# SBUF pools in another order, three small tiles filled up: where the matmul operands begin

## Chip, core and metric

The kernel runs on one core of one Trainium2 chip. Its time is the device time of one execution in microseconds (us), and a profiled execution gives a trace of the same program. TensorE is called PE here, and PEld is its loading of the stationary operand; VectorE is DVE, ScalarE is ACT, GpSimd is POOL, SyncE is SP.

## What is computed

One layer of a hybrid encoder trunk, for 1024 positions and a width of 1024, in float32:

```python
h = rms_norm(x, pre_norm_gain)
q, k, v, z_a, b_gate, c_gate, u, z_c = split(h @ w_in, 8)        # 8 x 512 columns
weights = softmax(q1 k1 + bias) - lam * softmax(q2 k2 + bias)    # 4 heads, block-causal, ALiBi
attn = rms_norm(weights @ v, subln_gain) * 0.2 * ... * silu(z_a)
conv_out = b_gate * conv3(c_gate * u) * silu(z_c)
mixed = concat(attn, conv_out) @ w_out
x = x + rms_norm(mixed, post_norm_gain)
e = rms_norm(p @ w_ple_proj, ple_norm_gain)
out = x + sigmoid(x @ w_ple_gate) * e
```

## The kernel before

Everything is held transposed: features lie on the 128 partitions and positions along the free dimension, in two halves of 512. A float32 product is made from three matmuls of type float32r: each operand is split into a high part (a rounded copy) and a low part (what the copy lost), and `mm3` (lines 93 to 96) adds high x high, high x low and low x high in one PSUM bank. `product` (line 123) runs it over the eight tiles of the contraction, 24 matmuls of 512 columns into one bank. In these the weights `w` are the stationary operand and the activations move: `hT` (the normalised input) in the input projection, whose banks are named `pj`; `mT` (the mixed groups) and `x1` (the residual stream) in the output projection and the gate, whose banks are named `o`. In the v projection it is the other way round: a slice of `hT` is stationary and the weights `wv` move, into `v`. Scores (`s`) have `qs` stationary and `ks` moving, in 256, 384 or 512 columns; `values` transposes the softmax weights on PE (`tpw`) and multiplies them as the moving `wt` with the stationary `vs` into `av`. `ple` is the projection of the per-layer embedding at the start.

The program has four parts in time. First x, p and the embedding weights are loaded and split and `ple` is made. Then come the first head's q and k and the v projection, whose results go through DRAM. Then, by the table `PLAN` and head by head, softmax on DVE and ACT alternates with further input projections on PE (gates and short convolutions). Last, `out_half` makes the output projection, `post_stat` and `post` the norm and the residual `x1`, half by half, and `gate_half` the gate and the output; the last `gate_half` goes in two pieces of 256 columns. DMAs are issued from SP; POOL makes the low parts of the weights (line 84). A scheduler orders the instructions of each engine from the order in which the code is written.

SBUF is given out by pools. A pool takes its place when it is opened, behind the pools that are open, and each tile takes its bytes per partition rounded up to a multiple of 32. So the start of a tile hangs on the sizes of all that lie before it. The pools, in the order of lines 49 to 55: `const` (identity, small constants, two rows `R` of scales), `hp` (16 buffers for hT, then mT, then x1), `mixp`, `tiny`, `rawp` (weights as loaded) and `wp` (weights split). Behind them the stages open and close their own: `qk` (qs, ks), `rowp`, `sp` and `s2` (wph, wpo, zero, pth, pto), `vp` (wv), `ap`, `a2` and `a3` (softmax weights, vs, wt), and in the last part `cp`, `c2`, `c4` and `wp2`. In `const`, before `hp`, lie tiles of 16, 64, 148, 4 and 128 bytes, which take 32, 64, 160, 32 and 128. In `mixp` the tile `gt` has 514 columns, 2056 bytes, and takes 2080; `lam_e` in `qk` has 8 bytes and takes 32.

Of the kernel before, what the change touches and what calls it, by code (L numbers as in the profile page):

```python
# [12 lines left out]
F32 = mybir.dt.float32  # L13
# [7 lines left out]
P = 128  # L21
# [4 lines left out]
HALF = 512  # L26
# [17 lines left out]
def hybrid_layer(ctx, tc, xT, pT, w_in, small, lams, w_out, w_ple, w_gate, outT):  # L44
    nc = tc.nc
    V, A, T, G = nc.vector, nc.scalar, nc.tensor, nc.gpsimd
    mult, add, sub = ALU.mult, ALU.add, ALU.subtract

    const = ctx.enter_context(tc.tile_pool(name="const", bufs=1))
    dram = ctx.enter_context(tc.tile_pool(name="dram", bufs=1, space=DRAM))  # L50
    hp = ctx.enter_context(tc.tile_pool(name="hp", bufs=16))
    mixp = ctx.enter_context(tc.tile_pool(name="mixp", bufs=1))
    tiny = ctx.enter_context(tc.tile_pool(name="tiny", bufs=3))
    rawp = ctx.enter_context(tc.tile_pool(name="rawp", bufs=3))
    wp = ctx.enter_context(tc.tile_pool(name="wp", bufs=3))
    ps_s = ctx.enter_context(tc.tile_pool(name="ps_s", bufs=3, space=PSUM))
    ps_a = ctx.enter_context(tc.tile_pool(name="ps_a", bufs=1, space=PSUM))

# [9 lines left out]
    ident = const.tile([P, P], F32, name="ident")  # L68
    make_identity(nc, ident)
    fold = const.tile([P, P], F32, name="fold")  # L70
    own = const.tile([P, 4], F32, name="own")
    nhalf = const.tile([P, 16], F32, name="nhalf")
    G.memset(nhalf, -0.5)
    sm = const.tile([P, 37], F32, name="sm")
# [67 lines left out]

    hT = operand("hT")
    mix = [[mixp.tile([P, HALF], F32, tag="mix", bufs=16, name=f"mix{k}_{n}") for n in range(2)] for k in range(KT)]
    gt = mixp.tile([P, HALF + 2], F32, name="gt")
    R = [const.tile([P, HALF], F32, name=f"R{n}") for n in range(2)]

    with ExitStack() as st:
        qk = st.enter_context(tc.tile_pool(name="qk", bufs=1))
        rowp = st.enter_context(tc.tile_pool(name="rowp", bufs=3))  # L150

        lam_in = mix[5][1][:, 0:256].rearrange("p (a b) -> p a b", a=4)
        lam_e = qk.tile([P, 2], F32, name="lam_e")
        nlam = qk.tile([P, 1], F32, name="nlam")

        def mixing_weight():
# [458 lines left out]
```

## Time and profile before

| | |
|---|---|
| median of three executions | 669.23 us (667.34 to 671.49) |
| the profiled execution | 670.35 us |
| its span, first to last instruction | 668.5 us |
| mean granted clock of TensorE in it | 0.992 of 2.4 GHz |

The span is what the trace shows; the profiled execution's own time is 1.85 us above it. Busy times are sums over the span for each engine. A matmul's end in the trace is modelled, and consecutive matmuls overlap there, so starts are to be read, not durations. The granted clock is 1.00 at 2.4 GHz and 0.50 at 1.2 GHz.

### The profile page before, as it was taken

What the parts mean: (1) busy time and instruction counts of PE and PEld (TensorE: products, weight loads), DVE (VectorE), ACT (ScalarE), POOL (GpSimd) and SP (SyncE); (2) the same over time, 40 slices, a digit from 0 to 9 for tenths busy, and PEclk for the clock granted to TensorE, in tenths of its full rate; (3) what the DMA queues carried; (4) which work ended last, traced back from release to release, by engine and by line L of the source; (5) the groups of instructions that cost most, each with busy time, mean ns of one, the idle gap of its engine ahead of it and who ended that gap; (6) DMA issues with size and microseconds to landing.
All of it is one profiled execution on the core that took longest, in us unless ns stands there. A gap on an engine that the chain in (4) does not pass through costs nothing.

```text
span 668.5 us, 8063 instructions
## 1 busy us (share of the span) xinstructions
PE 651.3 (97%) x2941; PEld 526.7 (79%) x2941; DVE 454.6 (68%) x828; ACT 241.7 (36%) x434; POOL 228.3 (34%) x115
## 2 busy tenths in 40 slices
PE   8999699999999999999999999999999999999996
PEld 5787478888888888888888888888888888877885
DVE  6959661479778786598834989618792189796333
ACT  6934441243443332344323334312541227231111
POOL 2046340032622354152351312425370187560000
PEclk9999899999999999999999999999999999999998
DMA  8966562300135001250012610113141024142222
GB/s 289 403 223 188 183 202 94 127 32 32 48 85 152 32 31 49 54 151 33 33 63 51 169 33 32 50 32 108 63 158 32 1 94 163 57 132 91 96 94 94
DMA packets 35654, 67.77 MB, mean 101 GB/s; under 512 B 3744, under 2 KB 12448, under 8 KB 35616
## 3 DMA queue, kind: packets, MB, share of 16 engines
q1 hardware_dynamic: 35616, 67.27, 30.7%
q8 instruction: 23, 0.38, 0.2%
q14 instruction: 15, 0.12, 0.1%
HBM read 48.38 MB, written 12.58 MB: 91 GB/s over the span
## 4 chain that ended last, share of the span: by engine, by line
PE 67%; DMA 11%; DVE 10%; issue 6%; POOL 5%; ACT 1%; SPq 0%; DVEq 0%; POOLq 0%
PE pj L94 12%; PE pj L96 12%; PE pj L95 12%; PE o L94 5%; PE o L96 5%; PE o L95 5%; PE s L232 5%; DMA e<-e_dram 4%; DMA out_dram<-e 3%; PE tpw L259 2%; POOL w L84 2%; PE v L94 2%; PE v L95 2%; PE v L96 2%; DMA mix<-in_xT 2%
## 5 line engine op out<-in xcount | busy, mean ns | idle before, releaser
L94 PE MATMUL pj<-hT,w 128*128 128x512 f32 x448 | 179.1, 400 | 0.6 <-ACT w L83 0.4
L96 PE MATMUL pj<-hT,w 128*128 128x512 f32 x448 | 178.1, 398 | 0.0
L95 PE MATMUL pj<-hT,w 128*128 128x512 f32 x448 | 177.9, 397 | 0.0
L84 POOL TENSOR_TENSOR w<-raw,w 128x1024 fp32r<-128x1024 f32 x42 | 106.8, 2549 | 202.3 <-ACT w L83 190.4
L94 PEld LDWEIGHTS pj<-hT,w 128*128 128x128 f32 x448 | 84.3, 188 | 19.3 <-ACT w L83 0.8
L96 PEld LDWEIGHTS pj<-hT,w 128*128 128x128 f32 x448 | 84.2, 188 | 18.6
L95 PEld LDWEIGHTS pj<-hT,w 128*128 128x128 f32 x448 | 84.2, 188 | 18.0
L240 ACT ACTIVATE p<-p,nm 128x128 f32<-128x128 f32 (+7 forms) x64 | 49.4, 772 | 73.9 <-DVE nm L236 63.3
L83 ACT CAST w<-raw 128x1024 fp32r<-128x1024 f32 x44 | 45.8, 1047 | 51.3 <-issue 35.2
L95 PE MATMUL o<-x,w 128*128 128x512 f32 (+1 forms) x136 | 52.1, 383 | 1.5 <-DVE x L84 1.5
L94 PE MATMUL o<-x,w 128*128 128x512 f32 (+1 forms) x136 | 52.2, 385 | 0.0
L96 PE MATMUL o<-x,w 128*128 128x512 f32 (+1 forms) x136 | 51.9, 381 | 0.0
L94 PE MATMUL o<-mT,w 128*128 128x512 f32 x128 | 51.1, 399 | 0.0
L96 PE MATMUL o<-mT,w 128*128 128x512 f32 x128 | 50.4, 395 | 0.0
L95 PE MATMUL o<-mT,w 128*128 128x512 f32 x128 | 50.2, 392 | 0.0
L232 PE MATMUL s<-ks,qs 128*128 128x512 f32 (+2 forms) x192 | 46.6, 347 | 0.5 <-issue 0.5
L236 DVE CUSTOM_DVE_ANT_0 p<-s,bias 128x512 f32<-128x512 f32 (+3 forms) x64 | 34.7, 565 | 9.6 <-PE s L232 5.6
L546 DVE SCALAR_TENSOR_TENSOR e<-e,sm,re 128x512 f32<-128x512 f32 x16 | 16.2, 1015 | 35.9 <-DMA e<-e_dram 35.9
L232 PEld LDWEIGHTS s<-ks,qs 128*128 128x128 f32 x192 | 33.3, 188 | 6.2 <-issue 0.9
L83 ACT CAST wt<-tpw 128x512 fp32r<-128x512 f32 (+3 forms) x48 | 20.7, 478 | 45.1 <-PE tpw L259 44.9
L84 DVE TENSOR_TENSOR wt<-tpw,wt 128x512 fp32r<-128x512 f32 (+3 forms) x48 | 25.2, 551 | 16.4 <-ACT wt L83 16.1
L555 ACT ACTIVATE tg<-o 128x512 f32<-128x512 f32 (+1 forms) x17 | 9.7, 572 | 65.6 <-PE o L96 63.0
(139 smaller groups left out, 1134.0 us busy)
## 6 DMA issues: line engine op xcount, KB each, us to landing
raw<-in_w_in SPq DMA_DIRECT2D x32, 512.0 KB, 3.9
mix<-in_xT SPq DMA_DIRECT2D x16, 256.0 KB, 5.9
e_dram<-e SPq DMA_DIRECT2D x16, 256.0 KB, 5.2
mix<-e_dram SPq DMA_DIRECT2D x16, 256.0 KB, 3.5
ks<-ks SPq DMA_DIRECT2D x16, 256.0 KB, 3.6
v_dram<-v SPq DMA_DIRECT2D x8, 512.0 KB, 3.1
vs<-v_dram SPq DMA_DIRECT2D x32, 128.0 KB, 2.8
raw<-in_w_out SPq DMA_DIRECT2D x8, 512.0 KB, 3.3
```

Of the source, the lines that this page charges most:

```text
L83: A.copy(out=hi, in_=src)
L84: (lo_eng or V).tensor_tensor(out=lo, in0=src, in1=hi.bitcast(F32), op=sub)
L94: T.matmul(out=ps, lhsT=ah, rhs=bh, start=first, stop=False)
L95: T.matmul(out=ps, lhsT=ah, rhs=bl, start=False, stop=False)
L96: T.matmul(out=ps, lhsT=al, rhs=bh, start=False, stop=last)
L232: T.matmul(out=banks[m][:, :nn], lhsT=s.qs[:, m, qi], rhs=s.ks[:, m, part, c], start=part == 0, stop=part == 1)
L236: V.tensor_tensor_reduce(out=pr[m][:, c0:c0 + n], in0=banks[m][:, :n], in1=s.bias[:, b0:b0 + n], scale=-1.0, scalar=low[m], op0=add, op1=A ...
L240: A.activation(out=pr[m][:, :W], in_=pr[m][:, :W], func=AF.Exp, scale=-1.0, bias=low[m], accum_out=l[:, m:m + 1])
L259: T.transpose(out=tp[:, ii * P:(ii + 1) * P], in_=s.ws[ii][:, j * P:(j + 1) * P], identity=ident)
L546: V.scalar_tensor_tensor(out=e, in0=e, scalar=col(C_PLE, m), in1=re[n], op0=mult, op1=mult)
L555: A.activation(out=t, in_=ps, func=AF.Tanh, scale=0.5)
```

## The change

The pools `hp`, `wp` and `rawp` are opened first, before `const`, `mixp` and `tiny`; and three small tiles are allocated larger and used in part: `own` with 16 columns (4 used), `gt` with 528 (514 used), `lam_e` with 16 (2 used).

```diff
+    hp = ctx.enter_context(tc.tile_pool(name="hp", bufs=16))
+    wp = ctx.enter_context(tc.tile_pool(name="wp", bufs=3))
+    rawp = ctx.enter_context(tc.tile_pool(name="rawp", bufs=3))
     const = ctx.enter_context(tc.tile_pool(name="const", bufs=1))
     dram = ctx.enter_context(tc.tile_pool(name="dram", bufs=1, space=DRAM))
-    hp = ctx.enter_context(tc.tile_pool(name="hp", bufs=16))
     mixp = ctx.enter_context(tc.tile_pool(name="mixp", bufs=1))
     tiny = ctx.enter_context(tc.tile_pool(name="tiny", bufs=3))
-    rawp = ctx.enter_context(tc.tile_pool(name="rawp", bufs=3))
-    wp = ctx.enter_context(tc.tile_pool(name="wp", bufs=3))
...
-    own = const.tile([P, 4], F32, name="own")
+    own = const.tile([P, 16], F32, name="own")[:, 0:4]
...
-    gt = mixp.tile([P, HALF + 2], F32, name="gt")
+    gt = mixp.tile([P, HALF + 16], F32, name="gt")[:, :HALF + 2]
...
-        lam_e = qk.tile([P, 2], F32, name="lam_e")
+        lam_e = qk.tile([P, 16], F32, name="lam_e")[:, 0:2]
```

Every engine has the same instructions in the same order with the same waits as before; what differs is addresses. Where the operands of matmuls begin in a partition, in bytes past a multiple of 64:

| matmuls into | moving operand | before | after | stationary operand | before | after |
|---|---|---|---|---|---|---|
| pj | hT | 32 | 0 | w | 0 | 0 |
| o | mT, x1 | 32 | 0 | w | 0 | 0 |
| v | wv | 32 | 0 | hT | 32 | 0 |
| s | ks | 32 | 0 | qs | 32 | 0 |
| av | wt | 32 | 0 | vs | 32 | 0 |
| ple | pth, pto | 32 | 0 | wph, wpo | 32 | 0 |
| tpw | identity | 0 | 0 | softmax weights | 32 | 0 |
| ms (column sums) | part | 0 | 0 | fold | 0 | 0 |

Past a multiple of 128 bytes, `w` began at 64 and begins at 0; the moving operands of pj, o and v began at 32 and begin at 0. The row tiles of `const` and `mixp` (`R`, `mix`, `gt`) went from 32 to 64 past a multiple of 128, the large tiles of the stages' own pools from 32 or 64 to 0.

## Rows read from the trace of the kernel before

**Rows 1.** The page, busy time, share of the span and instructions of each engine
```profile
PE 651.3 (97%) x2941; PEld 526.7 (79%) x2941; DVE 454.6 (68%) x828; ACT 241.7 (36%) x434; POOL 228.3 (34%) x115
```

**Rows 2.** Who waited for whom, PE: us in total, times, longest us
```profile
PE v L94 <- DVE v L87: 2.6, 1, 2.6
PE o L95 <- DVE x L84: 1.5, 2, 0.7
```

**Rows 3.** Busy time by stretch: PE, PEld, DVE, ACT, POOL; PE clock, DMA share, GB/s
```profile
89.00:598.00 509.00, 508.86 (x2348) 416.93 (x2348) 356.84 (x689) 182.08 (x340) 189.53 (x87) 1.00 0.24 75
...
607.00:663.00 56.00, 55.84 (x263) 45.87 (x262) 20.83 (x32) 6.37 (x11) 0.00 (x0) 1.00 0.29 94
```

**Rows 4.** Timeline of PE, output projection: start us, us, engine, line
```profile
499.95 0.40 PE L94 MATMUL o<-mT,w 128*128 128x512 f32 x1
...
511.15 0.40 PE L94 MATMUL o<-mT,w 128*128 128x512 f32 x1
```

**Rows 5.** Timeline of PE, input projection
```profile
462.15 0.40 PE L94 MATMUL pj<-hT,w 128*128 128x512 f32 x1
...
473.35 0.40 PE L94 MATMUL pj<-hT,w 128*128 128x512 f32 x1
```

**Rows 6.** Timeline of PE, v projection
```profile
105.13 0.39 PE L94 MATMUL v<-wv,hT 128*128 128x512 f32 x1
...
110.57 0.39 PE L94 MATMUL v<-wv,hT 128*128 128x512 f32 x1
```

**Rows 7.** Timeline of PE, the last product, in pieces of 256 columns
```profile
656.92 0.28 PE L94 MATMUL o<-x,w 128*128 128x256 f32 x1
...
661.96 0.28 PE L94 MATMUL o<-x,w 128*128 128x256 f32 x1
```

**Rows 8.** Timeline of PE, v projection after its wait
```profile
81.05 0.63 PE L95 MATMUL v<-wv,hT 128*128 128x512 f32 x1
...
84.04 0.63 PE L96 MATMUL v<-wv,hT 128*128 128x512 f32 x1
```

**Rows 9.** Busy time by stretch, columns as in rows 3
```profile
81.00:84.00 3.00, 3.00 (x8) 2.31 (x7) 0.00 (x0) 0.09 (x1) 3.00 (x2) 0.50 0.90 283
...
500.00:511.00 11.00, 11.00 (x49) 8.86 (x48) 4.53 (x6) 2.17 (x4) 0.71 (x1) 1.00 0.18 61
462.00:474.00 12.00, 12.00 (x53) 9.68 (x52) 10.76 (x21) 5.19 (x9) 4.19 (x2) 1.00 0.38 132
```

**Rows 10.** Line 358, both operands 32 past: ns min/median/max
```profile
L358 DVE TENSOR_TENSOR R<-R,sqx x14: 676/683/693, 14.7 to 75.1; 128x512 f32<-128x512 f32 x14
```

**Rows 11.** Line 518, both operands on a multiple of 64
```profile
L518 DVE TENSOR_TENSOR acc<-acc,sqo x14: 677/692/2883, 501.8 to 574.0; 128x512 f32<-128x512 f32 x14
```

**Rows 12.** Groups of loads of the stationary operand: count, busy us, mean ns
```profile
L94 PEld LDWEIGHTS pj<-hT,w 128*128 128x128 f32 x448 | 84.3, 188 | 19.3 <-ACT w L83 0.8 <-DVE tq L189 0.6 <-ACT hT L86 0.3
...
L232 PEld LDWEIGHTS s<-ks,qs 128*128 128x128 f32 x192 | 33.3, 188 | 6.2 <-issue 0.9
```

**Rows 13.** PE on tile pj from 89 to 598 us: busy us (count), clock, DMA share, GB/s
```profile
89.00:598.00 509.00, 304.41 (x1200) 1.00 0.24 75
```

**Rows 14.** PE on tile o from 89 to 598 us: busy us (count), clock, DMA share, GB/s
```profile
89.00:598.00 509.00, 117.82 (x503) 1.00 0.24 75
```

**Rows 15.** PE on tile v from 89 to 598 us: busy us (count), clock, DMA share, GB/s
```profile
89.00:598.00 509.00, 33.12 (x144) 1.00 0.24 75
```

**Rows 16.** Groups of score matmuls of 512 columns: count, busy us, mean ns
```profile
L232 PE MATMUL s<-ks,qs 128*128 128x512 f32 x80 | 24.0, 397 | 0.0
```

**Rows 17.** Busy time by stretch, columns as in rows 3
```profile
363.00:396.00 33.00, 32.94 (x158) 27.02 (x158) 26.85 (x67) 14.23 (x32) 10.11 (x4) 1.00 0.38 107
396.00:429.00 33.00, 33.00 (x156) 27.07 (x155) 31.15 (x72) 12.24 (x23) 10.25 (x5) 1.00 0.10 33
```

**Rows 18.** Timeline of PE, four scores between projections
```profile
392.53 1.09 PE L232 MATMUL s<-ks,qs 128*128 128x512 f32 x4
393.46 0.39 PE L94 MATMUL pj<-hT,w 128*128 128x512 f32 x1
```

## The prediction

> **What bounds the kernel now.** I read the busy table first, then the waits of TensorE (PE), then stretches of the program, then the start times of single matmuls. The busy table has PE at 97% of a 668.5 us span, VectorE at 68%, ScalarE and GpSimd near a third [rows 1]. What PE waits for is short; the waits that matter here are 2.6 us for the first v and 1.5 us for the split of x1 [rows 2]. In the 509 us from 89 to 598 us PE is busy for 508.9 us with 2348 matmuls, and from 607 to 663 us for 55.8 of 56 us with 263, at a granted clock of 1.00, the 2.4 GHz level [rows 3]. So five sixths of the time is one row of matmuls behind another, and the time there is their number times the distance between two starts. That distance is the thing to look at. The 0.39 or 0.40 us that the profile gives as one matmul's duration overlaps its neighbours and says nothing of the pace.
>
> In the output projection, 48 matmuls of 512 columns go from 499.95 to 511.15 us, which is 11.20 / 48 = 233.3 ns each [rows 4]; the input projection does 48 from 462.15 to 473.35 us, the same 233.3 ns [rows 5]. The v projection needs 5.44 us for 24, 226.7 ns each [rows 6]. The last product, in 256 columns, takes 5.04 us for 42, 120.0 ns each [rows 7]. And in the stretch after PE's wait for the first v, seven of v's matmuls take 2.99 us, 427.1 ns each [rows 8], at a granted clock of 0.50, the 1.2 GHz level [rows 9].
>
> **What the pace says.** At 1.2 GHz a matmul costs 427.1 / 512 = 0.834 ns a column, one column per cycle with nothing lost. Half of it, 213.6 ns for 512 columns or 0.4171 a column, is what 2.4 GHz would give. The projections need 233.3 for 512 and 120.0 for 256: a slope of 113.3 / 256 = 0.4426 ns a column, 6.1% over 0.4171, plus a constant of 120.0 - 256 x 0.4426 = 6.7 ns. The v projection's 226.7 ns is that same slope with no constant (512 x 0.4426 = 226.6). So there are two losses, both absent at the lower clock: one that grows with the columns, 13 ns in 512, close to one column in sixteen, and sixteen float32 columns are 64 bytes; and a constant of 6.7 ns. In pj and o the moving operand (hT, mT, x1) begins 32 past a multiple of 64 bytes and the stationary one (w) on a multiple; in v (wv, hT) both begin 32 past, and v has no constant. The other engines don't make the difference: from 500 to 511 us VectorE is busy for 4.5 of 11 us, from 462 to 474 us for 10.8 of 12 [rows 9], and the pace is the same.
>
> **The change, part by part.** It adds and removes no instruction; the order on each engine and the waits are those of before. Only addresses move: the moving operands hT, mT, x1, wv, ks, wt and pth and the stationary hT, qs, vs and wph go from 32 past a multiple of 64 to a multiple, w stays on one. No transfer, queue or buffer count changes, and no step is moved past another.
>
> The other engines' operands move by 32 too, and I cost this at nothing. VectorE adds two 128x512 tiles in 683 ns (median) where both lie 32 past [rows 10] and in 692 ns where both lie on a multiple [rows 11]. Loading the stationary operand takes a mean of 188 ns both with w on a multiple and with qs 32 past it [rows 12], so the load alone isn't sensitive either.
>
> For the moving operand, the lower end in 512 columns is half the cold pace, 213.6 ns, and the upper end is today's 233.3; a worse pace is a rival below. In between lies v's 226.7. I take 217 ns, near the lower end: the loss by columns comes in steps of the size of the boundary, and it is there in both kinds of product, which share the moving operand's place and not the stationary one's; the constant is missing where both operands lie alike, as all will. The last 3.4 ns I leave, because at the lower clock a few ns per matmul may be hidden. The Trainium skill (TensorE: Matmul & The Clock Gate, section "Wait — 56ns, not 53.3ns?") gives back-to-back starts as the columns over the clock, plus about 2.5 ns at 2.4 GHz and plus nothing at 1.2: the cold row agrees (427.1 ns against its 426.7), the warm ones don't (226.7 and 233.3 against its 215.7). By that page's 215.7 the sum below would be some 3 us larger, an estimate.
>
> The sum, for the two stretches in which PE hardly waits. pj has 1200 matmuls from 89 to 598 us [rows 13]; o has 503 there [rows 14] and 263 from 607 to 663 us [rows 3], of which 48 in 256 columns (two pieces of 24), so 718 long ones: 1918 x (233.3 - 217.0) = 31.3 us. v has 144 [rows 15]: 144 x 9.7 = 1.4 us. The scores have 80 in 512 columns [rows 16] and av by the code 72, taken at the projections' pace (the scores' row agrees, below): 152 x 16.3 = 2.5 us. By the code 64 scores have 256 columns, as the 48 of o: 120.0 - (256 x 0.4171 + 3.4) = 9.8 ns each, 1.1 us; and 48 have 384, at 13 ns by the same slope and constant, 0.6 us. Together 36.9 us.
>
> What of it is lost. Before 89 us I count nothing: PE waits there for VectorE and ScalarE and would only wait longer. At 598 us PE waits for the split of x1 [rows 2], behind the column sums of the second half and `post(1)` on VectorE; meanwhile PE has the five products `gate_half(0..4, 0)`, 120 matmuls, which save 120 x 16.3 = 2.0 us and give it to that wait. From 363 to 429 us VectorE is busy for 26.85 + 31.15 = 58.0 of 66 us [rows 17]; PE at 217 would want to do that stretch in 66 x 217 / 233.3 = 61.4 us with VectorE 94% busy, and I take 3 us of waits there, bounds 0 and 6. Elsewhere from 89 us on VectorE has more room (356.8 of 509 us in all [rows 3]), and three w buffers and DMAs at a share of 0.24 keep covering the loads. So 36.9 - 2.0 - 3 = 31.9 us. The profiled execution took 670.35 us, its span 668.5; 670.35 - 31.9 = 638.4. The median of the three runs is 669.23, 1.1 lower, so I forecast **637 us**. Bounds: at 213.6 ns and with no waits of VectorE the sum is 36.9 + 3.4 x 2374 / 1000 = 45.0, less 2.4, so 627; with the constant of 6.7 ns staying (220.3 ns) it is 36.9 - 3.3 x 2.4 = 29, less 1.6 and 3, so 645, and with 6 us of waits 648.
>
> **The rivals.** First, only the constant goes: the loss by columns belongs to float32 at the full clock, whatever the address, and all that matters is that the two operands lie alike. For it: v lies alike and has no constant, 32 past as it is. Against it: the scores lie alike as well, and four of them take 0.93 us, 232.5 ns each [rows 18]; but they stand in short runs among pj's, which leaves it open. Then pj and o come to 226.7: 1918 x 6.6 = 12.7 us, scores and av 1.0, the short ones 0.9, less 0.8 at 598 us and 1 for VectorE, so 13 us and 656 us.
>
> Second, the change doesn't do what it says: neither loss hangs on addresses. For it: the stationary load and VectorE show no effect of the same 32 bytes [rows 10 to 12]. Against it: the difference of v from pj and o, for which I find no other cause. It gives 669 us. The Trainium skill (SBUF — State Buffer, section "Specifications (TRN2)") gives SBUF lines of 16 bytes; by this rule an operand 32 past a multiple of 64 begins on a line already, and nothing would change. No operand here lies off 16 bytes, so no run shows it.
>
> Third, on the other side, slower: the next stationary operand is loaded during each matmul, and with both operands on multiples of 64, nearly all of them on multiples of 128, the two reads meet at the same place, so that the constant is paid twice: 1918 x 6.7 = 12.9 us, and v pays it once, 144 x 6.7 = 1.0, so 683 us. It decides as soon as the pace of pj passes 233.3 ns. Against it: v, where both lie alike, is the fastest.
>
> **How the numbers follow.** Both losses gone or nearly so: 0.55, 637 us, its own range 627 to 648. Only the constant: 0.18, 656 us. No change: 0.17, 669 us. Slower: 0.10, 683 us. A range that holds 8 of 10 takes in the first two and most of the third and leaves out the slower case and a little below: 627 to 669.5 us. Within 1% (about what a measurement of this kernel can tell from no change) is the third case, 0.17; faster by more 0.73; slower by more 0.10.
>
> **What the changed profile would show.** Right: pj's and o's matmuls in 512 columns start every 214 to 220 ns, v's at the same pace as they; the cold stretch still at 427; VectorE's durations as before; PE's waits at 598 us and around 363 to 429 us longer. If pj comes down to v's 226.7 and v stays, the first rival holds; at 233.3 the second; above it, the third. The forecast is also wrong if the pace falls but PE then waits for VectorE in many stretches, or if the longer wait near 598 us lets the granted clock fall to 0.50 there, as it did after the waits before 81 us: the seven matmuls in 3 us [rows 8] would have taken half of that.

## The result and the profile after

The changed kernel takes 661.24 us (median of four executions, 659.91 to 662.53) against 668.79 us for the kernel before on the same chip (four, 667.34 to 671.49): a ratio of 0.9882 with a 95% interval from 0.9844 to 0.9921, 1.2% or about 7.6 us faster. The forecast was 637 us. The profiled execution took 661.78 us, its span is 659.9 us. Behind the pools that are opened at the start, lines of the kernel stand two further down than before.

First the busy table, the first lines of the page of the kernel after, against [rows 1]:

```profile
span 659.9 us, 8063 instructions
## 1 busy us (share of the span) xinstructions
PE 641.5 (97%) x2941; PEld 525.9 (80%) x2941; DVE 453.3 (69%) x828; ACT 241.7 (37%) x434; POOL 227.7 (35%) x115
```

Then stretches of the kernel after that answer to [rows 3]; the columns are the busy time of PE, PEld, DVE, ACT and POOL with their counts, the granted clock, the DMA share and GB/s.

```profile
88.00:590.00 502.00, 501.65 (x2349) 416.83 (x2348) 356.17 (x688) 181.57 (x339) 189.44 (x87) 1.00 0.24 76
...
599.00:655.00 56.00, 55.16 (x262) 45.84 (x261) 21.26 (x33) 6.76 (x12) 0.00 (x0) 1.00 0.29 96
```

PE does 2349 matmuls in 502 us where 2348 took 509. VectorE's work is what it was, 356.2 us against 356.8 in the stretch of [rows 3]. So the gain lies in PE's pace, and the starts show where. From the timeline of PE in the kernel after (start us, us, engine, line): 48 matmuls of the input projection; 24 of the output projection with a weight tile in one of `wp`'s three buffers; 24 with a tile in one of `wp2`'s five; 24 of the v projection; 42 of the last product.

```profile
455.87 0.39 PE L98 MATMUL pj<-hT,w 128*128 128x512 f32 x1
...
466.75 0.39 PE L98 MATMUL pj<-hT,w 128*128 128x512 f32 x1
...
512.00 0.39 PE L96 MATMUL o<-mT,w 128*128 128x512 f32 x1
...
517.45 0.40 PE L96 MATMUL o<-mT,w 128*128 128x512 f32 x1
...
545.35 0.40 PE L96 MATMUL o<-mT,w 128*128 128x512 f32 x1
...
550.94 0.39 PE L96 MATMUL o<-mT,w 128*128 128x512 f32 x1
...
101.70 0.39 PE L96 MATMUL v<-wv,hT 128*128 128x512 f32 x1
...
107.14 0.39 PE L96 MATMUL v<-wv,hT 128*128 128x512 f32 x1
...
648.25 0.28 PE L96 MATMUL o<-x,w 128*128 128x256 f32 x1
...
653.28 0.28 PE L96 MATMUL o<-x,w 128*128 128x256 f32 x1
```

pj: 10.88 / 48 = 226.7 ns, against 233.3 in [rows 5]. o: 5.45 / 24 = 227.1 with `wp`, but 5.59 / 24 = 232.9 with `wp2`, hardly less than the 233.3 of [rows 4]. v: 5.44 / 24 = 226.7, exactly [rows 6]. The 256 columns: 5.03 / 42 = 119.8, [rows 7] again. So the change took 6.6 ns off most of pj and off some of o, and nothing off what was at 226.7 already.

What sets the two groups of o apart is in the allocation. The moving mT and x1 start 128 past a multiple of 256 bytes. So do `wp`'s three buffers; `wp2`'s five, behind `c4`, start on a multiple. I grouped all successive warm starts of both traces in 512 columns by the distance between the starts of the stationary and the moving operand, modulo 256 bytes, and took means ("alike" is distance 0; how the few longer distances among them are treated moves a mean by up to 0.8 ns):

| | before | after |
|---|---|---|
| pj | 160 apart, 233.6 ns | alike, 228.5 ns |
| o, w in `wp` | 160 apart, 233.4 | alike, 227.6 |
| o, w in `wp2` | 160 apart, 233.4 | 128 apart, 232.5 |
| v | alike, 227.0 | alike, 227.4 |
| scores | alike, 232.6 (234.7 before a pj) | alike, 229.7 |
| av | alike, 231.9 | alike, 227.5 |

So being alike isn't the whole of it: the scores and av lay alike before too, and were slow. In the kernel after, all the operands in the table except the w of `wp2` start 128 past a multiple of 256; before, those of scores and av started 32 past, and among them stood the matmuls of pj, whose w started 192 past.

Of PE's waits in the kernel after these answer to [rows 2] (engine, line, what it waited for: us in total, times, longest); of those not shown none is over 1.2 us, and the 1.2 us one at the very start was there before:

```profile
PE ms L112 <- DVE part L105: 3.4, 1, 3.4
PE v L96 <- DVE v L89: 2.4, 1, 2.4
PE o L97 <- DVE x L86: 1.7, 3, 0.7
```

Last, the last stage, which the prediction had counted as PE's. Towards its end the chain of waits of the kernel before turns in a ring; one turn, in its longest pieces (start us, us, what):

```profile
642.60 0.75 DVE e L546
643.35 0.61 DVE e L557
643.98 2.01 DMA out_dram<-e
646.01 2.56 DMA e<-e_dram
648.68 0.75 DVE e L546
```

The last turn in the kernel after:

```profile
646.37 0.75 DVE e L548
647.12 0.61 DVE e L559
647.75 1.99 DMA out_dram<-e
649.76 2.56 DMA e<-e_dram
652.44 0.75 DVE e L548
```

There is no PE in it. `gate_half` has three buffers for `e`. VectorE waits in order for a loaded e and scales it; behind that stands the add that finishes an older e; only when that e is written out is its buffer free for the next load. One turn takes 648.68 - 642.60 = 6.1 us before and 652.44 - 646.37 = 6.1 after. PE needs 24 x 233.3 = 5.6 us for the product that goes with it, so by this chain it wasn't the bound there even before. In the kernel after it is busy for 55.16 of 56 us there, and still its last matmul starts 6.0 us before the end of the span (before: 55.84 of 56 us, and 5.9 us).

For the experiments I cut the span at two matmuls, counted from 0 in the order of their starts: 305 (early in the v projection) and 2690 (past the wait for the split of x1).

| | start to 305, us | 305 to 2690 | 2690 to end | span |
|---|---|---|---|---|
| before | 89.1 | 520.5 | 58.9 | 668.5 |
| after | 87.7 | 513.6 | 58.6 | 659.9 |

The change is worth 6.8 us in the middle, 1.4 at the start and 0.4 at the end.

### The profile page after: what moved, and what is told of

Read it like the earlier page. It is cut to its first block, busy times and chain, and to the rows that moved or that the text cites. A ratio compares the mean times of both kernels' runs of the same rounds, so it can differ in the third digit from the quotient of the medians.

```text
span 659.9 us, 8063 instructions
## 1 busy us (share of the span) xinstructions
PE 641.5 (97%) x2941; PEld 525.9 (80%) x2941; DVE 453.3 (69%) x828; ACT 241.7 (37%) x434; POOL 227.7 (35%) x115
## 4 chain that ended last, share of the span: by engine, by line
PE 59%; DVE 16%; DMA 9%; issue 7%; POOL 5%; ACT 3%; DVEq 0%; SPq 0%; POOLq 0%
PE pj L96 12%; PE pj L97 11%; PE pj L98 11%; PE s L234 4%; DMA e<-e_dram 3%; DMA out_dram<-e 3%; DVE mix L536 3%; PE o L98 3%; PE o L96 3%; PE o L97 3%; PE tpw L261 2%; POOL w L86 2%; PE v L96 2%; DVE x L86 2%; PE v L97 2%
## 5 line engine op out<-in xcount | busy, mean ns | idle before, releaser
L96 PE MATMUL pj<-hT,w 128*128 128x512 f32 x448 | 177.2, 395 | 0.9 <-DVE tq L191 0.5
L98 PE MATMUL pj<-hT,w 128*128 128x512 f32 x448 | 176.3, 394 | 0.0
L97 PE MATMUL pj<-hT,w 128*128 128x512 f32 x448 | 176.1, 393 | 0.0
L548 DVE SCALAR_TENSOR_TENSOR e<-e,sm,re 128x512 f32<-128x512 f32 x16 | 16.3, 1016 | 35.5 <-DMA e<-e_dram 35.5
```

The source lines that it names most:

```text
L96: T.matmul(out=ps, lhsT=ah, rhs=bh, start=first, stop=False)
L97: T.matmul(out=ps, lhsT=ah, rhs=bl, start=False, stop=False)
L98: T.matmul(out=ps, lhsT=al, rhs=bh, start=False, stop=last)
L548: V.scalar_tensor_tensor(out=e, in0=e, scalar=col(C_PLE, m), in1=re[n], op0=mult, op1=mult)
```

## Experiments

The theory that the trace suggests: what counts is how the two operands of a matmul lie to each other, and alike they start every 226.7 ns (the first rival's mechanism; the expectations call it theory A). Against it stand the prediction's own reading (the moving operand's multiple of 64 matters; theory B), and that something else in the new layout did it. A time in brackets is that of the kernel before on the same chip.

**Everything alike** (`e1_w_alike`): the kernel after with 128 unused bytes ahead of `wp2`.

```diff
         c4 = st.enter_context(tc.tile_pool(name="c4", bufs=4, reuse_waits="tile"))
+        gap = st.enter_context(tc.tile_pool(name="gap", bufs=1))
+        gap.tile([P, 32], F32, name="gap_t")
         wp2 = st.enter_context(tc.tile_pool(name="wp2", bufs=5, reuse_waits="tile"))
```

> The changed kernel with an unused 128 bytes ahead of wp2, so that all eight weight buffers begin alike with the moving operand modulo 256 bytes (in the changed kernel five of the eight are 128 off). Theory A, the pace hangs on where the stationary operand begins relative to the moving one: the o matmuls on wp2's tiles come from a mean of 232.5 to 227 ns, about 480 x 5.5 = 2.6 us, so about 658.6 us against 661.2. Theory B, only the multiple of 64 matters, and the slow o products have another cause: 661 us, o's mean stays mixed.

All 733 distances of o in 512 columns now have a mean of 227.0 ns, those with `wp2` too; two products of the output projection from its timeline, 5.44 us each:

```profile
539.72 0.39 PE L98 MATMUL o<-mT,w 128*128 128x512 f32 x1
...
545.16 0.39 PE L98 MATMUL o<-mT,w 128*128 128x512 f32 x1
...
550.60 0.39 PE L98 MATMUL o<-mT,w 128*128 128x512 f32 x1
```

The time is 660.68 us (before 668.86; ratio 0.9877, 0.9861 to 0.9893), the same as the change's within the intervals. The last matmul starts 3.9 us earlier than after, 2.1 of them because the start is shorter, 0.9 in the middle (the products with `wp2` save 1.8 there, and the wait for the split of x1 takes back 1.0) and 0.9 in the last stage. The span ends only 0.9 earlier: the tail behind the last matmul is 9.0 us instead of 6.0. The chain of waits shows why:

```profile
631.29 0.75 DVE e L550
632.04 0.61 DVE e L561
632.67 1.99 DMA out_dram<-e
634.68 4.43 DMA e<-e_dram
639.24 0.75 DVE e L550
...
645.46 0.75 DVE e L550
...
651.55 0.75 DVE e L550
```

The last turn of e is still 6.1 us (651.55 - 645.46), and one turn took 8.0, because its load took 4.43 us where the others take 2.6. With 24 x 226.7 = 5.4 us for a product PE gains a lead there that the end doesn't see.

**Alike, but 32 past** (`e2_all_32_past`): the kernel before with 96 unused bytes ahead of `wp`, so that w starts 32 past a multiple of 64, as hT does.

```diff
     rawp = ctx.enter_context(tc.tile_pool(name="rawp", bufs=3))
+    gap = ctx.enter_context(tc.tile_pool(name="gap", bufs=1))
+    gap.tile([P, 24], F32, name="gap_t")
     wp = ctx.enter_context(tc.tile_pool(name="wp", bufs=3))
```

> The kernel before with an unused 96 bytes ahead of wp: hT, mT and x1 stay 32 past a multiple of 64, and w goes to 32 past as well, alike modulo 256. In the later stages wv, ks, qs, wt and vs go to a multiple of 64, so in v the moving operand is on a multiple and the stationary hT is 32 past. Theory A: pj and o at 227 ns although 32 past, v from 227 up to about 233; about 659.5 us. Theory B: pj and o stay at 233.3, v no slower; about 668 us.

664.9 us (before 668.86; 0.9939, 0.9916 to 0.9962). pj, alike, has 229.0 ns and o 227.0 on operands 32 past: the multiple of 64 isn't needed. v got slower, 233.5 ns, with its moving wv now on a multiple of 64 and its stationary hT 160 bytes off it: the multiple of 64 isn't enough either. Two of v's matmuls, 48 apart, 11.20 us:

```profile
104.86 0.40 PE L96 MATMUL v<-wv,hT 128*128 128x512 f32 x1
...
116.06 0.40 PE L96 MATMUL v<-wv,hT 128*128 128x512 f32 x1
```

The time is behind what I expected because v, scores (233) and av (232 to 234) gained nothing or lost, because the wait for the split of x1 grew from 1.5 to 2.9 us, and because of the tail (8.4 us, one load of e at 3.3 us).

**The multiple of 64 for the moving operand, w 160 off** (`e3_mov_aligned_w_off`): the kernel after with gaps ahead of `wp` and `wp2`, without the larger small tiles.

```diff
+    gap = ctx.enter_context(tc.tile_pool(name="gap", bufs=1))
+    gap.tile([P, 40], F32, name="gap_t")
     wp = ctx.enter_context(tc.tile_pool(name="wp", bufs=3))
...
+        gap2 = st.enter_context(tc.tile_pool(name="gap2", bufs=1))
+        gap2.tile([P, 48], F32, name="gap2_t")
         wp2 = st.enter_context(tc.tile_pool(name="wp2", bufs=5, reuse_waits="tile"))
```

> The changed kernel with w moved to 32 past a multiple of 64 by 160 unused bytes: every moving operand still begins on a multiple of 64 bytes, and w stands to hT, mT and x1 as in the kernel before (160 further, modulo 256). Theory A: pj and o back at 233.4 ns, about 669 us, with v (192 off) perhaps slower than 227. Theory B (the moving operand's multiple of 64 is what helps): pj stays near 227, about 661 us.

670.37 us, ratio 1.0015 (0.9999 to 1.003): nothing is gained. hT, mT and x1 start where they start in the kernel after, and pj is at 233.8, o at 233.4; two of pj, 48 apart, 11.20 us:

```profile
462.64 0.40 PE L98 MATMUL pj<-hT,w 128*128 128x512 f32 x1
...
473.84 0.40 PE L98 MATMUL pj<-hT,w 128*128 128x512 f32 x1
```

This takes the moving operand's own start out of the question.

**The pace by distance** (`m1_offsets`). This kernel and the two other m kernels leave the layer out: they copy x into the two operands and run series of matmuls into one bank, with a chosen start for either operand. Each ran once, at a granted clock of 1.00. A series, in short:

```python
def series(name, m0, s0, n=HALF, w=P, reps=36, mt=mov, stt=sta):
    bank = ps.tile([P, HALF], F32, tag="b", bufs=2, name=name)
    for i in range(reps):
        m, s = m0 + 1024 * (i % 3), s0 + 512 * (i % 4)
        T.matmul(out=bank[:w, :n], lhsT=stt[:, s:s + w], rhs=mt[:, m:m + n], start=i == 0, stop=i == reps - 1)
    ...
series("da", 0, 0)
...
series("dg", 0, 16)
...
series("dm", 0, 64)
...
series("nc", 0, 0, n=256)
...
series("bf", 0, 0, mt=movb, stt=stab)
```

> Leaves the layer out: loads eight tiles of x, writes them to the output, and runs series of 36 matmuls that differ in one thing each. Series da to dm: 512 columns of float32r, stationary start 0, 4, 8, 16, 32, 48, 64, 96, 128, 160, 192, 224, 256 bytes past the moving one. aa, ab, ac: both 16, 32, 64 past. Theory A: da, dm and aa to ac 226.7 ns, the others up to 240. Theory B: da, dg, di, dk, dm and ac alike, the rest slower. For what is left of the loss where both are alike: if a fixed part per matmul goes to the load of the stationary operand, 384 and 256 columns (nb, nc) need 173.3 and 120.0 ns, 64 and 32 stationary columns (wb, wc) about 220 and 217 in 512; if it grows with the columns, one in sixteen, nb and nc need 170.0 and 113.3 and wb, wc stay at 226.7. bfloat16 (bf, 512 columns): 213 to 220 by either.

Five of its 25 series in the timeline, one row for 36 matmuls (start us, us from the first start to the last end): operands alike, 64 bytes apart, 256 bytes apart, alike in 256 columns, alike in bfloat16.

```profile
25.58 8.33 PE L73 MATMUL da<-mov,sta 128*128 128x512 f32 x36
...
75.61 8.55 PE L73 MATMUL dg<-mov,sta 128*128 128x512 f32 x36
...
125.83 8.32 PE L73 MATMUL dm<-mov,sta 128*128 128x512 f32 x36
...
164.93 4.47 PE L73 MATMUL nc<-mov,sta 128*128 128x256 f32 x36
...
193.86 7.94 PE L73 MATMUL bf<-movb,stab 128*128 128x512 bf16 x36
```

Means of the last 24 distances between starts of each series in 512 columns, ns, by how many bytes the stationary operand starts past the moving one:

| 0 | 4 | 8 | 16 to 64 | 96 | 128 | 160 | 192 | 224 | 256 |
|---|---|---|---|---|---|---|---|---|---|
| 226.7 | 232.5 | 230.7 | 233.3 | 234.2 | 232.6 | 233.3 | 228.9 | 233.3 | 226.7 |

With both operands 32 or both 64 bytes past a multiple of 128 it is 226.7, with both 16 past it 230.0. By length, alike: 512 columns 226.7, 384 173.3, 256 120.0, 128 111.7. Half the cold pace of [rows 8] is 213.6, 160.2 and 106.8 for the first three: the loss is 13 ns at each of these lengths, a fixed amount and no loss by columns. At 128 columns it is far more (53.4 would be half the cold pace), so something else bounds those; what, no run here shows. In bfloat16 the paces are 215.8 and 109.2 for 512 and 256 columns, a loss of 2.2 and 2.4. The Trainium skill (TensorE: Matmul & The Clock Gate, section "Wait — 56ns, not 53.3ns?") has the columns over the clock plus about 2.5 ns; the bfloat16 series agree, the float32r ones don't. Fewer stationary columns, operands alike, were expected at 217 to 227 ns and came out slower: 64 of them 230.0, 32 of them 231.7.

**The e buffers** (`e6_changed_e5bufs`, `e4_w_alike_e5bufs`): the kernel after, and the first experiment, with five buffers for e. Theory C in the expectations is that the ring of e became the bound of the last stage in the first experiment, with its faster products; theory D that the late end there has another cause.

```diff
-            e = c4.tile([P, HALF], F32, tag="e", bufs=3, name="e")
+            e = c4.tile([P, HALF], F32, tag="e", bufs=5, name="e")
```

> The changed kernel with five buffers for e and nothing else. Theory C: its matmuls of the gate stage are slow enough to hide that chain, so little moves, 660.5 to 661.2 us; the two edits together (e4) give more than the sum of each alone. Theory D: the same as the changed kernel.

> The kernel of e1_w_alike (all weight buffers alike with the moving operand) with five buffers for e in place of three. Theory C, in e1 the last matmul started 3.9 us sooner than in the changed kernel (650.0 against 653.9 us), but the end came only 0.9 us sooner, because the chain of e's output transfer, e's load and VectorE's scaling became the bound of the gate stage: with more buffers the last matmul still starts near 650 and the span ends 6 us later, near 656, so about 658 us. Theory D, the late end of e1 has another cause, such as the transfers themselves: no change against e1, 660.7 us.

The e chain is gone from the end of both. The last pieces of the chain of waits of the kernel after with five buffers:

```profile
651.71 0.12 PE o L96
651.95 0.13 PE o L98
652.10 0.39 ACT tg L557
652.52 0.44 DVE e L558
652.98 0.42 DVE e L559
```

From matmul 2690 to the end it takes 57.5 us instead of 58.6, and with all alike 56.6 instead of 60.7. So the ring had cost the kernel after 1.1 us as well, which I had expected its slower products to hide. (The scheduler, given the buffers, also moved some instructions of VectorE and SyncE.) The medians are 659.26 us (ratio 0.9864, 0.9846 to 0.9882) and 660.66 (0.9882, 0.9864 to 0.99), both against 669.02. The first is the fastest of all the runs, but its interval overlaps the change's, so I don't call it faster. With all alike the 658 us expected didn't come: the profiled execution took 658.95 us, the three others 660.6 to 660.8, and of those there is no trace. In the profiled one the scheduler had put PE's matmuls around 470 us in another order, a wait is new there, and 305 to 2690 takes 514.2 us instead of 512.7.

```profile
PE pj L96 <- DVE mix L430: 1.3, 1, 1.3
```

**The order of the pools alone** (`e5_order_alone`): the kernel after with `own`, `gt` and `lam_e` as small as before.

```diff
-    own = const.tile([P, 16], F32, name="own")[:, 0:4]
+    own = const.tile([P, 4], F32, name="own")
...
-    gt = mixp.tile([P, HALF + 16], F32, name="gt")[:, :HALF + 2]
+    gt = mixp.tile([P, HALF + 2], F32, name="gt")
...
-        lam_e = qk.tile([P, 16], F32, name="lam_e")[:, 0:2]
+        lam_e = qk.tile([P, 2], F32, name="lam_e")
```

> The pools in the changed order, without the three filled-up tiles. hT and the three buffers of wp are as in the changed kernel, ks, qs, wv, wt and vs begin 32 past a multiple of 256, so v's operands lie 96 apart, and wp2's five buffers lie 64 off the moving operand in place of 128. Theory A (relative place): pj as in the changed kernel, o as in it (64 costs what 128 costs), v up from 227 to about 233 (144 x 6 = 0.9 us), scores and av a little up where pj's loads lie among them (152 x 4 = 0.6 us): about 663 us. Theory B (multiples of 64): o better than in the changed kernel or as in it, s, av and v worse by 7 ns: 664 us.

665.74 us (before 669.02; 0.9955, 0.9939 to 0.997): 3.3 of the 7.6 us. hT and `wp` are alike, and pj has 229.1 ns; but wv is 96 off its hT and v goes to 234.2, w in `wp2` is 64 off (233.4), scores and av stay at 231 to 232, and a pj that is followed by a score or an av takes 234 to 235. The time is 2.7 us over the 663 expected; against the kernel after, the middle is 3.0 us longer, of which pj has 1.1, v 1.0, scores and av 0.7 and o 0.3. So the rest of the change's gain is the larger tiles' part.

**Which pair collides** (`m2_pairs`): series in which one start alternates between two places.

```python
series("xa", 0, 0, reps=48, alt=(32, 32))    # a matmul's own operands alike, the next stationary one 128 bytes off
series("xb", 0, 0, reps=48, alt=(32, -32))   # its own 128 off, the next stationary one alike
...
series("xe", 0, 0, reps=48, alt=(32, 0))     # only the moving one alternates
series("xf", 0, 0, reps=48, alt=(0, 32))     # only the stationary one
```

> Leaves the layer out: series of 48 matmuls, 512 columns of float32r, with x's tiles. xa: moving and stationary start alternate together between 0 and 128, so that a matmul's own two operands lie alike, and the moving operand and the stationary one of the next matmul, which is loaded meanwhile, lie 128 apart. xb: the stationary start alternates the other way round, own pair 128 apart, meanwhile-loaded pair alike. xc, xd: the same with 32 bytes. If the load of the next operand beside the moving one is what loses time, xb and xd need 226.7 ns and xa and xc 231 to 234; if a matmul's own pair decides, the other way round. xe, xf: only one of the two alternates, by 128: every second pair apart, 229 to 230 by both. wa to wj: 96, 64 and 32 stationary columns at several starts: where the load is alike in place, 64 columns need 220 and 32 need 217 if the fixed 13.3 ns of float32r go with the columns loaded; if the fixed part is the same whatever is loaded, none comes below 226.7.

228.3, 230.0, 230.0 and 233.3 ns; with 32 bytes in place of 128, xc and xd need 231.7 and 230.0. Neither the matmul's own pair nor the pair with the next stationary operand decides by itself, nor do the two together: in xf the pairs are those of xa and of xb in turn, and it is slower than both. Loading 96, 64 or 32 stationary columns instead of 128 gives 228.3 to 232.8, never less than 226.7, so the time isn't that of the load's length.

**All alike, all 32 past** (`e7_all_alike_32_past`): the first experiment with 32 bytes ahead of all pools.

```diff
+    lead = ctx.enter_context(tc.tile_pool(name="lead", bufs=1))
+    lead.tile([P, 8], F32, name="lead_t")
     hp = ctx.enter_context(tc.tile_pool(name="hp", bufs=16))
```

> The kernel of e1_w_alike with 32 unused bytes ahead of all pools: every moving and every stationary operand of pj, o, v, s and av begins 32 past a multiple of 64, none on one, and all of them alike modulo 256. Theory A (relative place): as e1, pj and o at 227 to 228.5 ns, 660.7 us. Theory B (the multiple of 64 that the change brings): back to 233, about 669 us.

661.34 us (before 667.51; 0.9897, 0.9875 to 0.9918), pj 228.5, o 226.9, v 227.3: as the first experiment, with no operand of these on a multiple of 64.

**What stands around a matmul counts too.** The layouts settle why the scores and av were slow although alike. The operands of av lie alike in all of them. Its mean in 512 columns is 227.5 or 227.6 ns where those of pj start at the same place modulo 256 (after, `e1_w_alike`, `e7_all_alike_32_past`), and 230.9 to 232.5 where they don't (before, `e2_all_32_past`, `e3_mov_aligned_w_off`, `e5_order_alone`). In the kernel after and in `e2_all_32_past`, av's own operands even start at the same 128 past a multiple of 256, and it takes 227.5 ns in one and 232.5 in the other; what differs on PE is the place of hT and w. How far back a neighbour counts is open.

**What the fixed part hangs on** (`m3_fixed_part`): series that repeat the base (pa), write the bank anew with each matmul (pb), use 64 of the 128 partitions (pc; pg with the operands 128 bytes apart), read one stationary tile (pd), one moving tile (pe), one of each (pf), take other lengths (ph 480, pi 448, pj 320 columns), or use bfloat16 with the operands alike (pk) and 32 and 128 bytes apart (pm, pn).

> Leaves the layer out: series of 48 matmuls with operands alike. For the 13.3 ns that are left at every length: if they belong to each load-and-matmul of float32r, then 480, 448 and 320 columns (ph, pi, pj) need 213.3, 200.0 and 146.7 ns, and a bank written afresh by every matmul (pb), 64 partitions of contraction (pc, pg), one stationary place (pd), one moving place (pe) or both (pf) stay at 226.7 in 512. If they come from accumulating in a bank, pb is faster; if from the bytes read in all partitions, pc and pg are; if from the change of address, pd to pf are. bfloat16 at other places (pm 32, pn 128 bytes off): 215.8 as alike (pk) if the loss by place belongs to float32r alone, up to 220 if not.

Rows of its timeline; in the bfloat16 series pk, pm and pn one of the 48 has no record:

```profile
25.52 11.04 PE L73 MATMUL pa<-mov,sta 128*128 128x512 f32 x48
36.40 11.04 PE L73 MATMUL pb<-mov,sta 128*128 128x512 f32 x48
...
80.38 11.04 PE L73 MATMUL pf<-mov,sta 128*128 128x512 f32 x48
...
130.17 10.53 PE L73 MATMUL pk<-movb,stab 128*128 128x512 bf16 x47
...
145.78 10.52 PE L73 MATMUL pm<-movb,stab 128*128 128x512 bf16 x47
```

pa, pb and pf: (11.04 - 0.39) / 47 = 226.6 ns. The last 24 distances of pc, pd and pe have 226.7 as well, and those of pg 232.7. Nothing of this kind touches it. bfloat16 keeps 215.8 whether its operands lie alike or not. 320 columns take 146.7, again 13 over half the cold pace; 480 and 448 take 216.7 and 206.7, 16 and 20 over where 13 was expected, for which I have no reason.

The middle of the span puts the runs in one row; it is free of the start's variation and of e, but holds the wait for the split of x1 (1.5 to 2.9 us):

| | 305 to 2690, us | 2690 to end |
|---|---|---|
| before | 520.5 | 58.9 |
| moving on a multiple of 64, w off | 520.8 | 61.2 |
| order of pools alone | 516.7 | 59.1 |
| pj and o alike, 32 past | 515.1 | 60.1 |
| after | 513.6 | 58.6 |
| all alike | 512.7 | 60.7 |
| all alike, 32 past | 512.6 | 60.6 |
| after, five e | 513.7 | 57.5 |
| all alike, five e | 514.2 | 56.6 |

## Why the prediction was right and wrong

Right were the sign, the place (the pace of the projections, with the other engines unchanged), and one of the two losses: the constant goes where both operands lie alike. That is the first rival's mechanism, held at 18%, with its 656 us nearer to the 661.24 than the 637 of the forecast. The stated range of 627 to 669.5 holds the 661.24 only because it takes in the rivals; the leading case's own 627 to 648 doesn't.

**The step that failed** is that the loss by columns hangs on the place ("comes in steps of the size of the boundary") and so would go with it, down to 217 ns. There is no loss by columns: alike, 256, 320, 384 and 512 columns all lose the same 13 ns. The slope of 0.4426 ns was drawn through 233.3 at 512 and 120.0 at 256 columns, both from o with its operands 160 apart. But 256 columns don't feel the distance: 120.0 apart in [rows 7], 119.8 alike after. The two points had different losses in them. v's 226.7 and the same 120.0 give (226.7 - 120.0) / 256 = 0.4168 ns, half the cold pace to a thousandth, and 13.3 fixed; that line was there to be drawn from [rows 6 to 8], and it leaves nothing for a place to take away from v. v, alike before as after, was the counterexample in hand: it had 226.7 ns and kept it, where the prediction put it at 217 as well. That its 226.7 fell on the wrong line with no constant (226.6) was chance. In the sum this step was 9.7 ns for each of 2214 long matmuls of pj, o, v, scores and av, 21 of the 36.9 us, and no run shows a mean float32r pace below 226.7 ns in 512 columns. The 5 us between the first rival's 656 and the 661.24 are about what pj's mean of some 2 ns over its best 226.7 (1200 x 2 = 2.4 us) and the w in `wp2` (2.7 us, next) come to.

**o went only in part.** The prediction took "on a multiple of 64" for "alike". w in `wp2` isn't: 128 apart, 471 distances with a mean of 232.5 ns. In the first experiment they have 226.8, so they are worth 5.7 ns each, 2.7 us. The allocation shows the 128 bytes, but only to one who compares the two starts.

**The last stage had no gain to give.** 215 long matmuls there were counted at 16.3 ns, 3.5 us. The chain of e, 6.1 us a turn against PE's 5.6, sets the end before and after; the prediction read PE busy for 55.8 of 56 us [rows 3] as PE being the bound. With five buffers for e the chain is gone and the stage takes 57.5 and 56.6 us, which shows it for the kernel after and for the one with all alike; for the kernel before it is read from the chain alone.

**Waits.** The 3 us of waits for VectorE from 363 to 429 us didn't come but for one new wait of 0.4 us; PE's pace there gained some 2% and not 7. The wait for the split of x1 was to take back 2.0 us and took 0.2 by the profile's rows (1.7 after against 1.5 [rows 2]; 0.4 by the starts), and 2.7 us is the wait with all alike. Scores and o gained at most 0.6 ns in 256 columns and the scores 1.2 ns in 384, where 1.7 us had been counted. Costing VectorE's moved operands and the load at nothing held: 453.3 us against 454.6 busy, and the stationary load still 188 ns.

**What adds up.** PE's matmuls stand in the same order in both kernels, so the distances between starts can be compared one by one. From 305 to 2690, 1153 distances of pj give 5.3 us (233.4 to 228.8 ns), o 1.4 (203 with `wp` 1.1, 327 with `wp2` 0.3), scores and av in 512 columns 0.6, all shorter ones 0.2: 7.5 us. The distances over 300 ns, the waits among them, give back 0.7, of which the split of x1 has 0.4. That leaves the 6.8. Before 89 us the prediction counted nothing and the trace has 1.4; but that start takes 85.5 to 88.7 us in the changed layouts, shortest where one wait is short (`ms` for DVE, 1.1 to 3.8 us), so I don't put it down to the change.

The second rival, no change, falls: the interval leaves out 1, and v can be slowed by moving it apart. The third, a collision where both lie on the same place, is wrong the other way round: same place is the fast case.

## What to carry to other kernels

Fit a pace only through matmuls that share every other property, and try each point against half the cold pace before naming a loss: one line here would have told a fixed cost from a loss by columns. For float32r products in 512 columns, look at the distance between the stationary and the moving operand's starts modulo 256 bytes, for every buffer of every pool, rather than at each operand's own multiple, and put products that alternate on PE at the same place. And a PE that is busy need not be the bound of a stage: follow the chain of waits there, and compare one turn of it with PE's product.

## What the runs showed of the hardware

- A row of float32r matmuls in 512 columns whose operands all start a multiple of 256 bytes apart: 226.7 ns each, with starts on a multiple of 64 bytes or 32 past one; with both 16 past one it is 230.0, so not every common start will do. 16 to 160 bytes apart it is 232.6 to 234.2, 192 apart 228.9, and 4 bytes are enough for 232.5. In o's 256 columns there is no difference (120.0 and 119.8), and in bfloat16 none at 32 and 128 bytes (215.8).
- A matmul whose operands lie alike is slower among neighbours that lie elsewhere: av takes 227.5 ns in the kernel after and 232.5 in `e2_all_32_past`, with its own operands at the same place modulo 256.
- Alike, a float32r matmul costs a fixed 13 ns over half the cold pace in 256, 320, 384 and 512 columns. It stays with one operand tile read over and over, with a fresh bank each time and with 64 partitions; with fewer stationary columns it is no smaller (230.0 to 231.7 ns in 512). At 448 and 480 columns it is 20 and 16. Where it comes from is open.
- That the distance matters looks like two reads that meet in SBUF, but this is argued only: the alternating series (228.3, 230.0, 230.0, 233.3) fit neither pair. The Trainium skill (TensorE: Matmul & The Clock Gate, section "Step-by-step: what each phase is for") says that loading the next weights takes no read bandwidth from the running matmul, since PE has two independent read ports; by that rule the distance would cost nothing. Here the measurement decides: for float32r it costs 6.6 ns of 233.3.
- In the chain of waits of the last stage one load of e took 4.2 to 4.4 us instead of 2.6 in three of the layouts; why is open.
